# A hybrid encoder layer: chunks of the delta recurrence issued beside the projections of queries and values, with the pages dealt out anew

## The chip, the cores and the metric

The kernel runs on one core of a Trainium2 chip. The metric is the time of one execution of the whole layer in microseconds (us), the median of several runs. Five engines work side by side, each through its own instructions strictly in the order in which they stand: TensorE (PE in the profile, with its weight loads as PEld), VectorE (DVE), ScalarE (ACT), GpSimd (POOL) and SyncE (SP), which here only issues transfers.

## The reference

One encoder layer over 1024 positions of width 1024, in float32. A common RMS norm and one projection feed two mixers: attention over a band of chunks (8 heads of 64) and a gated delta recurrence (4 heads of 128). Their outputs go through an output projection, then a feed-forward network follows.

```python
u    = rms_norm(h, mix_norm_gain)
aq, ak, av, dqkv, dgate, da, db = split(u @ w_in)
o_att = rms_norm(chunked_rel_attention(aq, ak, av, ...), att_out_gain)
dq, dk, dv = split(silu(causal_conv4(dqkv)))
# the recurrence, per head and chunk of the sequence:
#   value, k_cumdecay = triangular solves with (I + strict(beta k k^T * decay))
#   v_new = value - k_cumdecay @ S
#   o     = q_decay @ S + attn_intra @ v_new
#   S     = S * chunk_decay + k_tail^T @ v_new
o_dn = rms_norm(o, dn_out_gain) * silu(dgate)
h = h + concat[o_att, o_dn] @ w_out
h = h + relu(rms_norm(h) @ w_ff1)**2 @ w_ff2
```

The recurrence is serial: chunk c + 1 needs the state S that chunk c leaves.

## The kernel before

The sequence is cut into 8 tiles of 128 positions (the kernel's recurrence also works on 8 chunks of 128). Float32 operands of the large products are split into a high and a low part and multiplied in three passes (`mm3`, L158), so one projection tile `proj_N` or `proj_T` is 24 matmuls of 512 columns.

Generators write the work, and `interleave` (L254) draws from them by weights: each step that a generator yields has a cost in made-up units, and the generator with the least cost per weight so far goes next. This is only the order in which the code is written. A scheduler of the framework then places the instructions on each engine; it may shift them, but within a pool of pages it hands out pages in the order in which the code asked for them.

The mixer has these generators:

- `delta_proj` for the recurrence's queries and values (dq, dv; convolution and SiLU on VectorE, results stored in DRAM), `gate_proj` (g), and `att_proj` for the attention's keys, queries and values (ak, aq, av). In `att_proj`, ScalarE squares a tile, VectorE reduces it, GpSimd takes a power for the norm, VectorE writes the normed tile `qn` (named ak0_n, ak1_n ...), TensorE transposes it (ak0_tp ...), ScalarE and VectorE split it and it is stored. A tile's bank of PSUM (three in `ps_a`) is free again once `qn` is written.
- `delta_prep` (L482): per chunk the products k k^T (d0_m ...), and at the end of all chunks a substitution of 31 steps on VectorE (`td`, `xd`) that inverts the 32x32 diagonal blocks. `xd` and its transposed copy `ad` are stored in DRAM as `x_dr` and `y_dr`.
- `delta_merge` (m0 ... m7) reads them back and builds each chunk's inverse Y by a chain of small products.
- `delta_state` (c0_tpv, c0_pk, c0_pv, c0_pq, c0_pS): the serial part of a chunk. `delta_out` and `delta_fin` (c0_Ltd, c0_tpq, c0_mt, c0_po, c0_tpo): its output.
- `attention` (tiles t00 to t07 for heads 0 to 3, t10 to t17 for heads 4 to 7; a tile is two pairs of heads): `score` (t_sb, t_sa), exponentials on ScalarE, `value` (transposes t_tpb and t_tpa, copies, products t_o), `finish` and `turn`.

Before the change, the first `interleave` (L1263) holds all projections, six of the eight tiles of attention values and `delta_prep`. The second (L1267) holds the attention, the whole recurrence `delta_all` and the last two tiles of values. The output projection `out_proj` follows, with the splits `mixed(0)` tied behind the last square of the recurrence, and the feed-forward network (`ff1`, `ff2`).

All pages of 512 columns live in pools by tag, used in turn: for instance `cv` has 5 pages, `dk` 8, `raw` 2, `x` 2, `on` 2, `u` 24 (the normed input), `wh` and `wl` 10 each.

Of the kernel before, what the change touches and what calls it, by code (L numbers as in the profile page):

```python
# [35 lines left out]
ORDER = "OSMOSMFSOMOSMSL"  # L36
LATE = 2
RS = "a"
NV = 6
WV = 2.5  # L40


@with_exitstack
def hymba_kernel(
# [208 lines left out]

    def interleave(*gens):  # L254

        done = [0.0] * len(gens)
        live = set(range(len(gens)))
        while live:
            i = min(live, key=lambda k: done[k])
            g, w = gens[i]  # L260
            try:
                done[i] += next(g) / w
            except StopIteration:
                live.discard(i)

    def load_block(col, name):
# [128 lines left out]

    def att_proj(u, col, kind, res=None):
        w = load_block(col, f"wa{kind}")
        for t in range(NT):
            n = f"a{kind}{t}"
            ps = proj_N(u[t // TPH], w, t % TPH, n + "_ps")  # L400
            if kind == "v":
                vs = page("jg", n + "_s")
                nc.scalar.mul(vs, ps, r_col[:, t:t + 1])
                nc.sync.dma_start(out=v_dr[t], in_=vs)
                res.append(vs)
                yield 5200
                continue
            sq = page("jq", n + "_sq")
            nc.scalar.activation(sq, ps, AF.Square, scale=r_col[:, t:t + 1])
# [3 lines left out]
            nc.gpsimd.tensor_scalar(r, r, r_col[:, t:t + 1], None, ALU.mult)  # L413
            qn = page("jv", n + "_n")
            q3 = qn.rearrange("p (h d) -> p h d", d=ATT_D)
# [4 lines left out]
            for i in range(4):  # L420
                nc.tensor.transpose(tp[:, i * P:(i + 1) * P], qn[:, i * P:(i + 1) * P], ident)
            hi = page("jg", n + "_h", F32R)
            lo = page("dk", n + "_l", F32R)
# [165 lines left out]
    def delta_state(c, ab, kTs, Ys, D):  # L589

        n = f"c{c}"
        T = "wh" if c + 1 < NT else "jv"
        h4 = slice(4 * c, 4 * c + 4)
# [40 lines left out]
    def delta_out(c, ab, kTs, D):  # L634
        n = f"c{c}"
        T = "wh" if c + 1 < NT else "cv"
        h4 = slice(4 * c, 4 * c + 4)
# [58 lines left out]

    def attention(after):


        def bias_page(tag, name):  # L700
            b = page(tag, name)
            nc.gpsimd.tensor_copy(b[:, 0:1], after[:, 0:1])
            return b
# [17 lines left out]
        def load_keys(g, hf):  # L721
            for i in range(4):
                h = 4 * g + i
                tag = (("dk", "dk"), ("dk", "wl")) if not g else (("u", "wl"), ("dk", "dk"))
                k = page(tag[hf][i // 2], f"ks{g}{hf}{i}", F32R)
                nc.sync.dma_start(out=k.bitcast(F32), in_=k_dr[h // 2, h % 2, :, TH * hf:TH * hf + TH])
                keys[g][hf].append(k)

        def load_values(ts):
            for t in ts:  # L730
                tl = page("dk" if t < 2 else "wl", f"vt{t}")
                nc.gpsimd.tensor_copy(tl[:, 0:1], after[:, 0:1])
                nc.sync.dma_start(out=tl, in_=v_dr[t])
                vt.append(tl)

        def load_rest():
            load_old(0)
            load_values((2, 3))
            load_keys(0, 1)
            load_values(range(4, NT))  # L740
# [154 lines left out]
        for i in range(len(units) + lag + late):  # L895
            if i < len(units):
                g, t, pp = units[i]
                if pp == 0:
                    start(g, t)
                    if (g, t) == (0, 2):  # L900
                        load_rest()
                    if (g, t) == (0, 6):
# [355 lines left out]
    for _ in delta_proj(u, DK, 4, "dk", None, kT, w_dk, first):  # L1258
        pass
    ab = ab_proj(u)  # L1260
    after = []
    values = att_proj(u, AV, "v", after)
    interleave(  # L1263
        (chained(delta_proj(u, DQ, 0, "dq", dq_dr), delta_proj(u, DV, 8, "dv", dv_dr), gate_proj(u),
                 att_proj(u, AK, "k"), att_proj(u, AQ, "q"), first_steps(values, NV)), 1.0),
        (delta_prep(kT, ab), 0.35))
    interleave((attention(after[NV - 1]), 1.0), (delta_all(ab, kT), 2.0), (values, WV))  # L1267
    R = out_proj()
# [51 lines left out]
```

## Time and profile before

| what | us |
|---|---|
| median of the runs (1318.3 to 1320.27) | 1318.68 |
| the profiled execution | 1318.95 |
| its span, first to last instruction | 1317.2 |
| PE busy in the span | 1268.3 |
| DVE busy | 913.0 |
| ACT busy | 543.0 |
| POOL busy | 329.2 |
| start of ak0 (keys' projection) | 214.3 |
| first score of the attention (t00) | 346.7 |
| first score of its second half (t10) | 443.5 |
| first matmul of the output projection | 572.7 |
| start of the feed-forward network's first product | 683.4 |

A matmul's record in the trace is longer than its turn on the array, since matmuls overlap: what one costs is the step from its start to the start of the next. A busy PE may therefore still lose time, by steps that are longer than the shape needs. PEclk is the granted share of TensorE's clock in a stretch, as a fraction of 1.

### The profile page before, as it was taken

How to read it: one execution, taken by the hardware profiler on the slowest of the kernel's cores; microseconds unless marked ns; L12 is line 12 of the kernel's file. 1: busy time of each engine (PE TensorE's matmuls, PEld its weight loads, DVE VectorE, ACT ScalarE, POOL GpSimd, SP SyncE). 2: the span in 40 equal slices, each digit the busy share in tenths (PEclk: the TensorE clock that was granted, in tenths of full speed). 3: DMA queues.
4: the chain of work that ended last, by engine and by line, in shares of the span. 5: the costliest groups of instructions: out<-in, count | busy, mean ns of one | idle time of the engine just before them, and what ended most of it. 6: DMA issues, size and time to landing. Idle time of an engine off the chain costs nothing.

```text
span 1317.2 us, 18003 instructions
## 1 busy us (share of the span) xinstructions
PE 1268.3 (96%) x6686; PEld 1045.9 (79%) x6686; DVE 913.0 (69%) x1379; ACT 543.0 (41%) x902; POOL 329.2 (25%) x513
## 2 busy tenths in 40 slices
PE   8999999999999998989988999999998999999998
PEld 6778878788888877868866888888887788888886
DVE  7899979554056565853549745565559898897988
ACT  7232222232266563744225434444456353333331
POOL 4426542543123364524335000000001000000032
PEclk9999999999999999989988999999999999999999
DMA  7214354666574432115241333323379433403002
GB/s 218 71 43 142 93 157 121 152 161 160 186 208 131 130 101 65 55 51 165 81 160 49 112 96 98 117 92 109 107 266 341 141 136 96 144 32 112 17 32 96
DMA packets 128791, 159.58 MB, mean 121 GB/s; under 512 B 22720, under 2 KB 71872, under 8 KB 128192
## 3 DMA queue, kind: packets, MB, share of 16 engines
q1 hardware_dynamic: 111296, 137.47, 33.7%
q10 hardware_dynamic: 17408, 20.98, 5.1%
q8 instruction: 52, 0.85, 0.3%
q14 instruction: 35, 0.29, 0.1%
HBM read 111.22 MB, written 47.19 MB: 120 GB/s over the span
## 4 chain that ended last, share of the span: by engine, by line
PE 74%; DVE 7%; DMA 2%; issue 2%; POOL 2%; ACT 1%; DVEq 0%; SPq 0%; ACTq 0%; POOLq 0%
PE q L1046 21%; PE p L1132 20%; PE op L163 7%; PE aq_ps L163 3%; PE av_ps L163 3%; PE t_o L850 3%; PE g_ps L163 3%; PE ak_ps L163 2%; DMA t_q<-q_dr 1%; PE t_tpa L840 1%; PE t_tpb L829 1%; PE t_sb L777 1%; PE t_sa L777 1%; DVE h L1013 1%; PE c_po L452 1%
## 5 line engine op out<-in xcount | busy, mean ns | idle before, releaser
L1174 POOL TENSOR_TENSOR y<-y,y 128x1024 f32<-128x1024 f32 x6 | 18.0, 3024 | 279.4 <-DVE y L1170 260.7
L1113 POOL TENSOR_TENSOR y<-y,y 128x1024 f32<-128x1024 f32 x2 | 6.4, 3201 | 294.7 <-DMA y<-h_dr 294.7
L1170 DVE TENSOR_TENSOR y<-y,p 128x1024 f32<-128x1024 f32 x50 | 60.2, 1215 | 12.1 <-PE p L1132 10.7
L793 DVE CUSTOM_DVE_ANT_0 t_pb<-t_sb,biasn 128x256 f32<-128x256 f32 (+1 forms) x64 | 25.6, 402 | 56.7 <-PE t_sb L778 30.9
L163 PE MATMUL op<-mh,wo_h 128*128 128x512 f32 x128 | 50.3, 393 | 0.2 <-DVE t_nm L802 0.2
L163 PE MATMUL op<-ml,wo_h 128*128 128x512 f32 x128 | 50.1, 392 | 0.0
L163 PE MATMUL op<-mh,wo_l 128*128 128x512 f32 x128 | 48.5, 391 | 0.0
L808 ACT ACTIVATE t_pb<-t_pb,t_nm 128x256 f32<-128x256 f32 (+1 forms) x64 | 31.6, 494 | 23.4 <-DVE t_nm L802 15.0
L850 PE MATMUL t_o<-t_ta,vt 128*64 128x128 f32 x240 | 30.1, 302 | 1.8 <-DVE t_ta L843 1.1
L802 DVE CUSTOM_DVE_ANT_0 t_pa<-t_sa,biaso,t_nm 128x384 f32<-128x384 f32 (+2 forms) x48 | 26.3, 548 | 5.5 <-PE t_sa L778 3.3
L163 PEld LDWEIGHTS op<-mh,wo_h 128*128 128x128 f32 x128 | 24.1, 188 | 5.8 <-PE t_tpo L456 0.6
L163 PEld LDWEIGHTS op<-mh,wo_l 128*128 128x128 f32 x128 | 24.0, 188 | 5.2 <-issue 0.2
L954 POOL TENSOR_TENSOR op_q<-op_q 128x512 f32<-128x512 f32 x14 | 19.9, 1422 | 32.7 <-ACT op_q L953 25.2
L777 PE MATMUL t_sb<-ks,t_q 128*128 128x256 f32 (+1 forms) x72 | 23.2, 333 | 5.0 <-DMA t_q<-q_dr 5.0
L163 PEld LDWEIGHTS op<-ml,wo_h 128*128 128x128 f32 x128 | 24.0, 188 | 4.8
L947 DVE TENSOR_TENSOR h<-op,op_x 128x512 f32<-128x512 f32 x16 | 10.8, 686 | 23.7 <-PE op L163 23.7
L298 PE MATMUL dk_ps<-uh,wdk_h 128*128 128x512 f32 x56 | 21.8, 414 | 5.5 <-ACT uh L180 5.5
L840 PE MATMUL t_tpa<-ident,t_pa 128*128 128x128 f32 x120 | 22.4, 293 | 4.5 <-ACT t_on L878 3.2
L811 ACT ACTIVATE t_pa<-t_pa,t_nm 128x384 f32<-128x384 f32 (+2 forms) x48 | 26.4, 550 | 0.1
L163 PE MATMUL g_ps<-uh,wg_l 128*128 128x512 f32 x64 | 25.2, 397 | 0.5 <-POOL wg_l L145 0.5
L850 PEld LDWEIGHTS t_o<-t_ta,vt 128*64 128x64 f32 x240 | 18.1, 144 | 9.5 <-issue 2.2
L163 PE MATMUL dq_ps<-uh,wdq_h 128*128 128x512 f32 x64 | 25.4, 397 | 0.0
(1103 smaller groups left out, 4438.8 us busy)
## 6 DMA issues: line engine op xcount, KB each, us to landing
wa<-in_w_ff_dram SPq DMA_DIRECT2D x32, 512.0 KB
a<-in_w_ff_dram SPq DMA_DIRECT2D x32, 512.0 KB
b<-f_dr SPq DMA_DIRECT2D x32, 512.0 KB
t_q<-q_dr SPq DMA_DIRECT2D x32, 256.0 KB
f_dr<-yy ACTq DMA_DIRECT2D x16, 512.0 KB
f_dr<-zz ACTq DMA_DIRECT2D x12, 512.0 KB
xt<-in_x_t_dram SPq DMA_DIRECT2D x16, 256.0 KB
ks<-k_dr SPq DMA_DIRECT2D x16, 256.0 KB
```

The source lines that it names most:

```text
L163: nc.tensor.matmul(ps, a, b, start=(i == 0), stop=(i == n - 1))
L298: nc.tensor.matmul(ps[ct], a[:, s], b, start=(k + m == 0), stop=(k == NKT - 1 and m == 2))
L777: nc.tensor.matmul(o, q[:, i * P:(i + 1) * P], k[:, c], start=True, stop=False)
L793: nc.vector.tensor_tensor_reduce(sb[:, c], bk[:, c], new[g][pp][:, c], -1.0, 3.0e38, ALU.add, ALU.min, nm[:, 4 + i:5 + i])
L802: nc.vector.tensor_tensor_reduce(sa[e][:, 0:wa], bk[:, 0:wa], old[g][i][:, 384 - wa:384], -1.0, nm[:, 4 + i:5 + i], ALU.add, ALU.min, nm[: ...
L808: nc.scalar.activation(sb[:, c], sb[:, c], AF.Exp, bias=m, scale=-1.0, accum_out=T["sums"][:, 4 + i:5 + i])
L811: nc.scalar.activation(sa[e][:, 0:wa], sa[e][:, 0:wa], AF.Exp, bias=m, scale=-1.0, accum_out=T["sums"][:, i:i + 1])
L840: nc.tensor.transpose(tp[:, js], sa[e][:, js], ident)
L850: nc.tensor.matmul(po[64 * e:64 * e + 64, pp * P:(pp + 1) * P], vt[k0 + j][:, 64 * h:64 * h + 64], (ta[e] if j < na else tb)[:, c:c + P], ...
L1046: nc.tensor.matmul(part(ps, q), l[:, s], r, start=(k + m == 0), stop=(k == 3 and m == 2))
L1132: nc.tensor.matmul(part(ps[q // 2], q % 2), l[:, s], part(r, k), start=(i + k + m == 0), stop=(i + k + m == 4))
L1170: nc.vector.tensor_tensor(y[i][m], y[i][m], ps[m], op)
```

## The change

The first `interleave` now holds `delta_prep` and `delta_all` as one chain with weight 0.4 (before: `delta_prep` alone with 0.35), and it ends as soon as the projections with four tiles of values are through (`until=0`). What is left of the recurrence goes on in the second one beside the attention, with weight 2.0 as before, and the four remaining tiles of values with weight 6 (before: two tiles, 2.5).

Pages are dealt out anew so that the recurrence can live beside the projections: `att_proj` no longer uses `jq`, `jv` and `jg`, which the recurrence needs, but `raw` (squares and values), `cv` (normed keys), `x` (normed queries) and `on` (high parts). Chunks 0 to 4 of the recurrence take their work pages from `dk` and not from `wh`. The first keys of the attention are read into pages of `u`. Some loads move from tile (0, 3) to (0, 2), and pages filled by a transfer are tied to the value tile 3 by a small page `mark`.

```diff
+EARLY = 5
-NV = 6
-WV = 2.5
+NV = 4
+WV = 6
...
-    def interleave(*gens):
+    def interleave(*gens, until=None):
...
                 live.discard(i)
+                if i == until:
+                    return
...
+    mark = mpool.tile([P, 1], F32, name="mark")
+
+    def att_proj(u, col, kind):
...
-                vs = page("jg", n + "_s")
+                vs = page("raw", n + "_s", w=516)[:, 0:512]
                 nc.scalar.mul(vs, ps, r_col[:, t:t + 1])
                 nc.sync.dma_start(out=v_dr[t], in_=vs)
-                res.append(vs)
+                if t == NV - 1:
+                    nc.gpsimd.tensor_copy(mark, vs[:, 0:1])
...
-            sq = page("jq", n + "_sq")
+            sq = page("raw", n + "_sq", w=516)[:, 0:512]
...
-            qn = page("jv", n + "_n")
+            qn = page("cv", n + "_n") if kind == "k" else page("x", n + "_n", w=SEQ)[:, 0:512]
...
-            hi = page("jg", n + "_h", F32R)
+            hi = page("on", n + "_h", F32R)
...
     def delta_state(c, ab, kTs, Ys, D):
-        T = "wh" if c + 1 < NT else "jv"
+        T = "dk" if c < EARLY else "wh" if c + 1 < NT else "jv"
...
     def delta_out(c, ab, kTs, D):
-        T = "wh" if c + 1 < NT else "cv"
+        T = "dk" if c < EARLY else "wh" if c + 1 < NT else "cv"
...
-                tag = (("dk", "dk"), ("dk", "wl")) if not g else (("u", "wl"), ("dk", "dk"))
+                tag = (("u", "u"), ("dk", "wl")) if not g else (("dk", "wl"), ("dk", "dk"))
...
         def load_rest():
-            load_old(0)
-            load_values((2, 3))
-            load_keys(0, 1)
             load_values(range(4, NT))
...
                     if (g, t) == (0, 2):
+                        load_old(0)
+                        load_values((2, 3))
+                        load_keys(0, 1)
+                    if (g, t) == (0, 3):
                         load_rest()
...
-    values = att_proj(u, AV, "v", after)
+    values = att_proj(u, AV, "v")
+    delta = chained(delta_prep(kT, ab), delta_all(ab, kT))
     interleave(
         (chained(delta_proj(u, DQ, 0, "dq", dq_dr), delta_proj(u, DV, 8, "dv", dv_dr), gate_proj(u),
                  att_proj(u, AK, "k"), att_proj(u, AQ, "q"), first_steps(values, NV)), 1.0),
-        (delta_prep(kT, ab), 0.35))
-    interleave((attention(after[NV - 1]), 1.0), (delta_all(ab, kT), 2.0), (values, WV))
+        (delta, 0.4), until=0)
+    interleave((attention(), 1.0), (delta, 2.0), (values, WV))
```

The instructions of TensorE are the same ones, in another order. Three places show it. A number behind a name tells instances apart; `x4` stands for four rows in a row that read alike, and a product of plain float32 operands (c0_pk, m0_p1 and the like) runs as two passes, so that its four rows are eight records in the trace.

The first place is TensorE behind the last matmuls of the fourth key tile (ak3). Before:

```order
L163 MATMUL ak3_ps_2474<-wak_7_h_2295,uh0_7_155 128x512
L163 MATMUL ak3_ps_2474<-wak_7_l_2296,uh0_7_155 128x512
L163 MATMUL ak3_ps_2474<-wak_7_h_2295,ul0_7_156 128x512
L421 MATMUL ak1_tp_2398<-ident_120,ak1_n_2396 128x128 x4
L163 MATMUL ak4_ps_2528<-wak_0_h_2253,uh1_0_157 128x512
```

The same place now:

```order
L164 MATMUL ak3_ps_2695<-wak_7_h_2403,ul0_7_156 128x512
L565 MATMUL m0_p1_2245<-m0_yb_2235,m0_ab_2234 32x32 x4
...
L581 MATMUL m0_tp_2267<-m0_yb_2235,m0_ab_2234 64x64 x4
L589 MATMUL m0_p4_2308<-m0_s1_2236 64x64 x4
L462 MATMUL c0_tpv_2322<-ident_120,c0_jv_2315 128x128 x4
L458 MATMUL c0_pk_2339<-state0_288,kT0_585 128x128 x4
...
L458 MATMUL c0_pv_2461<-c0_jv_2315,m0_yb_2235 128x128 x4
...
L458 MATMUL c0_pq_2479<-state0_288,c0_jq_2314 128x128 x4
...
L458 MATMUL c0_pS_2550<-c0_vn_2466,c0_kt_2320 128x128 x4
L427 MATMUL ak1_tp_2527<-ident_120,ak1_n_2525 128x128 x4
L164 MATMUL ak4_ps_2775<-wak_0_h_2361,uh1_0_157 128x512
```

Between the key tiles 3 and 4 now stand the merge of chunk 0, most of that of chunk 1, and the serial part of chunk 0; before, the first product of a merge came four key tiles later.

The second place is VectorE at the end of the substitution and behind it. Before, ak1_n stood between the last two steps:

```order
L534 TENSOR_TENSOR xd_1599<-xd_1599,td_1600 128x31
L416 TENSOR_TENSOR ak1_n_2396<-ak1_ps_2357,ak1_r_2391 128x512
L125 TENSOR_SCALAR ak2_v_2449<-ak2_ss_2447 128x8
L536 COPY ad_1598<-xd_1599 128x1024
L130 TENSOR_TENSOR ak2_t_2453<-ak2_y_2451 128x8
```

Now:

```order
L540 TENSOR_TENSOR xd_1513<-xd_1513,td_1514 128x31
L542 COPY ad_1512<-xd_1513 128x1024
...
L610 TENSOR_TENSOR c0_jv_2315<-c0_tpv_2322,br_794 128x512
L616 SCALAR_TENSOR_TENSOR c0_jv_2315<-c0_pk_2339,nbr_796,c0_jv_2315 128x128
L616 SCALAR_TENSOR_TENSOR c0_jv_2315<-c0_pk_2339,nbr_796,c0_jv_2315 128x128 x3
L629 TENSOR_TENSOR c0_o_2484<-c0_pq_2479,edec_792 128x512
L422 TENSOR_TENSOR ak1_n_2525<-ak1_ps_2486,ak1_r_2520 128x512
L422 TENSOR_TENSOR ak2_n_2615<-ak2_ps_2576,ak2_r_2610 128x512
```

The tile ak1_n, which frees the bank of ak1, now stands behind c0_o; both take a page of `cv`, and the code asks for that of c0_o first.

The third place is TensorE in the attention's second half, at tile t15. Before:

```order
L452 MATMUL c6_pS_5194<-c6_vn_5109,c6_kt_5005 128x128 x4
...
L777 MATMUL t15_sa1_6184<-ks101_3816,t15_q_6166 128x384
L778 MATMUL t15_sa1_6184<-ks101_3816,t15_q_6166 128x384
L456 MATMUL c7_tpv_5220<-ident_120,c7_jv_5213 128x128 x4
L456 MATMUL c6_tpq_5226<-ident_120,c6_jq_4999 128x128 x4
L829 MATMUL t14_tpb0_6137<-ident_120,t14_pb0_6033 128x128 x4
L840 MATMUL t14_tpa0_6144<-ident_120,t14_pa0_6047 128x128 x3
L452 MATMUL c7_pk_5248<-state1_289,kT1_644 128x128 x4
L840 MATMUL t14_tpa1_6150<-ident_120,t14_pa1_6052 128x128 x3
L456 MATMUL c5_tpo_5312<-ident_120,c5_o_4962 128x128 x4
```

Now:

```order
L780 MATMUL t15_sa1_6186<-ks101_4915,t15_q_6168 128x384
L781 MATMUL t15_sa1_6186<-ks101_4915,t15_q_6168 128x384
L832 MATMUL t14_tpb0_6139<-ident_120,t14_pb0_6035 128x128 x4
L843 MATMUL t14_tpa0_6146<-ident_120,t14_pa0_6049 128x128 x3
L843 MATMUL t14_tpa1_6152<-ident_120,t14_pa1_6054 128x128 x3
L853 MATMUL t14_o_6138<-t14_ta0_6150,vt0_4265 64x128
```

The recurrence is gone from here: its last instruction on TensorE, c7_tpo, now stands at the start of this half (between rows of t07_o), and before it stood at the last one, t17.

More of the change, by code (lines that the diff above doesn't have):

```diff
@@ L394, in ab_proj @@
         return dict(beta=beta, edec=edec, br=br, br2=br2, nbr=nbr, ned=ned, gh=gh.bitcast(F32), gl=gl)
-    def att_proj(u, col, kind, res=None):
+    mark = mpool.tile([P, 1], F32, name="mark")
+    def att_proj(u, col, kind):
         w = load_block(col, f"wa{kind}")
@@ L695, in delta_all, with attention @@
                 yield from gens[k]
-    def attention(after):
+    def attention():
         def bias_page(tag, name):
             b = page(tag, name)
-            nc.gpsimd.tensor_copy(b[:, 0:1], after[:, 0:1])
+            nc.gpsimd.tensor_copy(b[:, 0:1], mark)
             return b
@@ L731, in load_values @@
                 tl = page("dk" if t < 2 else "wl", f"vt{t}")
-                nc.gpsimd.tensor_copy(tl[:, 0:1], after[:, 0:1])
+                nc.gpsimd.tensor_copy(tl[:, 0:1], mark)
                 nc.sync.dma_start(out=tl, in_=v_dr[t])
@@ L1260, in hymba_kernel @@
     ab = ab_proj(u)
-    after = []
-    values = att_proj(u, AV, "v", after)
+    values = att_proj(u, AV, "v")
+    delta = chained(delta_prep(kT, ab), delta_all(ab, kT))
     interleave(
```

## The prediction

> **What bounds the kernel now.** I read the stretches first: busy time by stage, cut at landmarks of TensorE's queue. The columns are the stretch, its length, then busy time (and instructions) of PE, PEld, DVE, ACT and POOL, the granted clock, the DMA share and GB/s.
>
> ```profile
> 214.30:237.80 23.50, 22.34 (x101) 18.20 (x100) 22.07 (x57) 6.19 (x10) 8.27 (x7) 1.00 0.50 134
> 237.80:346.70 108.90, 108.90 (x526) 88.14 (x525) 46.30 (x104) 29.78 (x51) 41.12 (x45) 1.00 0.62 157
> 346.70:443.50 96.80, 95.78 (x884) 81.76 (x882) 51.29 (x184) 58.33 (x177) 36.05 (x104) 1.00 0.60 180
> 443.50:572.70 129.20, 114.20 (x1028) 97.77 (x1027) 80.53 (x237) 72.56 (x208) 62.01 (x154) 0.95 0.25 72
> 572.70:675.60 102.90, 100.15 (x478) 81.17 (x476) 45.18 (x63) 34.03 (x61) 39.30 (x36) 0.98 0.35 112
> ```
>
> The rows are: keys 0 to 3, with the substitution (`td`, `xd`) on DVE; the other keys, queries and values; the attention's first half; its second half; the output projection. TensorE looks busy everywhere, but records of matmuls overlap, so I take its work from steps instead, the timeline of TensorE giving the start of each row:
>
> ```profile
> 549.65 0.60 PE L456 MATMUL c_tpo<-ident,c_o 128*128 128x128 f32 x4
> 550.09 1.06 PE L452 MATMUL c_mt<-c_jq,kT 128*128 128x128 f32 x8
> 550.90 0.36 PE L777 MATMUL t_sa<-ks,t_q 128*128 128x256 f32 x1
> 551.10 0.28 PE L778 MATMUL t_sa<-ks,t_q 128*128 128x256 f32 x1
> 551.22 0.22 PE L777 MATMUL t_sa<-ks,t_q 128*128 128x128 f32 x1
> ...
> 552.45 0.76 PE L850 MATMUL t_o<-t_ta,vt 128*64 128x128 f32 x9
> 552.94 0.27 PE L850 MATMUL t_o<-t_tb,vt 128*64 128x128 f32 x1
> ```
>
> Four transposes step 0.44, so 0.11 each; eight records of a plain float32 product 0.81, so 0.10 (0.11 taken); 256 columns 0.12; nine value products 0.49, so 0.055. A wide matmul of 512 columns steps 0.22 to 0.23, by the rows around the fourth key tile (ak3), which the change touches first:
>
> ```profile
> 237.26 0.39 PE L163 MATMUL ak_ps<-wak_h,uh 128*128 128x512 f32 x1
> 237.48 0.39 PE L163 MATMUL ak_ps<-wak_l,uh 128*128 128x512 f32 x1
> ...
> 237.95 0.60 PE L421 MATMUL ak_tp<-ident,ak_n 128*128 128x128 f32 x4
> 238.30 0.48 PE L163 MATMUL ak_ps<-wak_h,uh 128*128 128x512 f32 x1
> ```
>
> TensorE's rows of each stage times these steps give its work there, in the order before and in the changed one (the recurrence's share in brackets):
>
> - keys 0 to 3, up to the first matmul of ak4 at 238.30: 22.7 (0) before, 30.5 (7.8) after;
> - the rest of the projections, up to t00: 105.2 (1.0), then 121.0 (27.6);
> - first half, up to t10: 79.6 (28.9), then 98.5 (36.9);
> - second half, up to the output projection: 90.6 (43.8), then 48.2 (1.3).
>
> The sum stays at 298. Before, the stages took 24.0, 108.4, 96.8 and 129.2 us, so 1.3, 3.2, 17.2 and 38.6 us are lost. Projections run at TensorE's pace; the attention with the recurrence beside it does not, above all its second half. The change moves recurrence from where 38.6 us are lost to where almost nothing is, so the sum asks how much of that loss goes and how much comes up among the projections.
>
> **The change part by part.**
>
> *The wait behind ak3.* The new order has, between ak3 and ak4, the merge m0 and chunk 0's first products. m0 needs the substitution's result, stored in DRAM and read back. That takes long before as well, but nobody waits for it there. DVE, SP and POOL, from their timelines:
>
> ```profile
> 235.47 0.18 DVE L534 TENSOR_TENSOR xd<-xd,td 128x31 f32<-128x31 f32 x1
> ```
> ```profile
> 236.41 2.77 SPq L539 DMA_DIRECT2D x_dr<-xd  x4
> ...
> 241.84 2.15 SPq L438 DMA_DIRECT2D k_dr<-ak_l  x2
> ...
> 247.92 1.31 SPq L438 DMA_DIRECT2D k_dr<-ak_l  x2
> 249.33 1.21 SPq L550 DMA_DIRECT2D m_s<-y_dr  x2
> ```
> ```profile
> 252.41 2.62 POOL L554 COPY m_yb<-m_s 32x128 f32<-32x128 f32 x8 [2.92 <-DMA m_s<-y_dr]
> ```
>
> `xd` ends at 235.65; SP issues stores and loads until 250.5; POOL's copies start at 252.41, released by the last load, and m0's four of eight are done at 253.7. Nothing on DVE ahead of this is moved, so `xd` ends when it did. On SP the two pairs of `ak_l` stores shown (2.15 + 1.31) fall behind the loads, because their tiles are late themselves: m0 can start at about 250.3. TensorE has its last matmul of ak3 done at 237.95 and then stands at m0_p1 for 12.4 us. Nothing can be put in: ak4 needs a bank of `ak_ps`, and `ak1_n`, which frees one, now stands on DVE behind `c0_o`, the end of chunk 0's first half, since both draw from `cv`. So m0 and chunk 0 must run through as one chain, with no projection in its holes. Its hops on other engines are a copy or an activation of at least the mean of the first row below (ACT, in the second half's groups) for each of m0's four, and DVE's `c_jv` twice and `c_o` (timeline of DVE; the last row is the chunk's state):
>
> ```profile
> L561 ACT COPY m_s<-m_p 32x128 f32<-32x128 f32 x6 | 1.5, 255 | 5.0 <-PE m_p L559 4.9
> ```
> ```profile
> 360.56 0.69 DVE L604 TENSOR_TENSOR c_jv<-c_tpv,br 128x512 f32<-128x512 f32 x1 [4.97 <-PE c_tpv L456]
> ...
> 363.22 1.13 DVE L610 SCALAR_TENSOR_TENSOR c_jv<-c_pk,nbr,c_jv 128x128 f32<-128x128 f32 x4 [0.46 <-PE c_pk L452]
> ...
> 369.85 0.69 DVE L623 TENSOR_TENSOR c_o<-c_pq,edec 128x512 f32<-128x512 f32 x1 [1.88 <-PE c_pq L452]
> ...
> 374.78 1.12 DVE L628 SCALAR_TENSOR_TENSOR state<-state,edec,c_pS 128x128 f32<-128x128 f32 x4 [1.33 <-PE c_pS L452]
> ```
>
> 1.0 + 2.5 = 3.5, with the hops' signals about 4. And a TensorE that stood so long restarts at half clock, as the end of the second half shows (a stretch; TensorE's timeline):
>
> ```profile
> 560.00:566.80 6.80, 4.23 (x16) 2.86 (x16) 3.02 (x8) 2.69 (x7) 4.13 (x13) 0.50 0.00 0
> ```
> ```profile
> 560.86 0.90 PE L840 MATMUL t_tpa<-ident,t_pa 128*128 128x128 f32 x3 [2.98 <-ACT t_on L878]
> 563.47 1.11 PE L456 MATMUL c_tpo<-ident,c_o 128*128 128x128 f32 x4 [1.71 <-POOL c_o L663]
> ```
>
> There 2.98 + 1.71 us of waiting kept the clock at 0.50 for 6.8 us, of which half, 3.4, is the most it can cost, and half of the busy 4.23, about 2, the least; I take 2.6. The term is 12.4 + 4 + 2.6 = **+19**. Low end 12: the chain's hops hidden and no clock loss. High end 26: copies as late as before (3.4 more) and the hops at twice 4 (with 3.4 for the clock, 27 in all, less what the transposes fill).
>
> The Trainium skill's page "TensorE: Matmul & The Clock Gate", Part 1, has the array at half rate after an idle window of about 3.4 us and full again after a busy one of as long. The trace's stretch is twice that length, being broken by a second wait. By the page alone the clock would cost 1.7 us instead of 2.6, and the sum would be 0.9 lower.
>
> *Queries, values and three chunks between them* (ak4 to t00). Each chunk's serial path has DVE's 0.69 + 1.13 + 0.69 + 1.12 = 3.6 us of the rows above. Covered by projection tiles of 24 x 0.227 = 5.4 us of matmuls they cost nothing; where TensorE's row behind is a dependent one, they stand bare. Chunks share `cv`, `dk` and `on` with keys and queries now, so `qn` and `hi` wait for pages as `ak1_n` does. Three chunks bare are 10.9, with one more fall to half clock 14; hidden, 0. Nothing in this stage of the trace shows which, so I take a little over half, **+8**.
>
> *First half* (t00 to t10). The loss of 17.2 falls on 39.8 us of attention and 28.9 of recurrence: 0.25 per us. The recurrence's 36.9 make that +2.0. The first scores' operands come at the end of the moved loads, and this wait is there already (the list of waits, second half: total, times, longest):
>
> ```profile
> PE t_sb L777 <- DMA t_q<-q_dr: 4.0, 2, 2.2
> ```
>
> one more of it is +2: **+4**. Low end −3: the two value tiles that move here from the stage ahead bring 10.9 us of matmuls without waits, which hide 10.9 x 0.25. High end +10: the loss in proportion to all the work, 21.3 (+4), a full 4.0 of the load's waits, and 2 for value rows still waiting for their pages.
>
> *Second half* (t10 to the output projection). Of TensorE's work 48.2 remain: 240 value products x 0.055, 216 transposes and the like x 0.11, 72 score products x 0.117 and 16 x 0.173. What it then waits for is ACT, whose work stays. ACT's timeline gives the steps of two exponentials (each has a read of its sum behind it), its groups in the second half the rest:
>
> ```profile
> 540.95 0.51 ACT L808 ACTIVATE t_pb<-t_pb,t_nm 128x256 f32<-128x256 f32 x1
> ...
> 541.46 0.60 ACT L811 ACTIVATE t_pa<-t_pa,t_nm 128x384 f32<-128x384 f32 x1
> ...
> 542.05 0.58 ACT L477 ACTIVATE c_po<-c_o 128x512 f32<-128x512 f32 x1
> ```
> ```profile
> L808 ACT ACTIVATE t_pb<-t_pb,t_nm 128x256 f32<-128x256 f32 (+1 forms) x31 | 15.3, 494 | 8.4 <-DVE t_nm L802 6.6 <-DVE t_nm L793 1.1 <-DVE t_tot L859 0.3
> L811 ACT ACTIVATE t_pa<-t_pa,t_nm 128x384 f32<-128x384 f32 (+2 forms) x23 | 12.6, 546 | 0.0
> L832 ACT COPY t_tb<-t_tpb 128x512 f32<-128x512 f32 (+1 forms) x16 | 8.9, 558 | 12.5 <-PE t_tpb L829 12.4
> ...
> L845 ACT COPY t_ta<-t_tpa 128x384 f32<-128x384 f32 (+2 forms) x12 | 5.0, 419 | 2.7 <-PE t_tpa L840 2.7
> ...
> L878 ACT ACTIVATE t_on<-t_on 128x512 f32<-128x512 f32 x6 | 3.6, 594 | 0.4 <-DVE t_on L873 0.4
> ...
> L869 ACT COPY t_pb<-t_o 128x256 f32<-128x256 f32 x8 | 2.9, 367 | 3.8 <-PE t_o L850 3.8
> ```
>
> 31 x 0.51 + 23 x 0.59 + 8.9 + 5.0 + 3.6 + 2.9 = 49.8 us. TensorE and ACT have nearly the same load and wait for each other in turn. To 49.8 I add the end, where nothing is left to lay between: the two waits, 4.7, and the half clock, 3.4; and some 2 for the splits of `mixed(0)` on ACT. That is 60 against 129.2, a loss of 11.8 instead of 38.6: **−27**. Low end: ACT's pace and 2 at the end, 52, so −35. High end: the loss rate of the first half on 46.8 of attention, 11.7, with the end's 8 and the splits' 2: loss 21.7, so −17.
>
> The output projection and all behind it keep their rows and order: 0. Sum: 19 + 8 + 4 − 27 = +4, against the profiled execution's 1318.95 (span 1317.2 and 1.75 around it), which lies 0.27 above the median: **1323**.
>
> **The rivals.**
>
> *Faster: the second half at ACT's pace, and chunks hidden among projections.* Speaking for it: ACT's idle time in the second half is in waits for TensorE's transposes and for DVE (L832's 12.5, L808's 8.4), which stand behind the recurrence's rows there and then no longer do. Against it: the same waits come up within a tile. With 52 there and 2 instead of 8 among the projections, the sum is 19 + 2 + 4 − 35 = −10: 1309. The point that decides, with the other terms as above, is a second half of 56 us. The Trainium skill's "Perfetto Trace Analysis", § Optimization Strategy, says that regimes with different contended engines may gain from being interleaved, which would be this case. The rows of the stages bear out that the regimes differ.
>
> *The gap is short.* If m0's operands were back within 5 us of ak3's end, the first term would be 5 and the time 1309. Against it stands SP's row of 14 us of issues and loads, of which the change takes only 3.5 away.
>
> *Slower by more: keys and queries themselves at the recurrence's pace.* Banks and pages freed by steps behind the chunk make each of them wait: the second term at 14, the first at 26, the rest as above, +20 with the first half at +7: 1339. The `ak1_n` place is one such already.
>
> *The change does nothing.* Excluded: the order moves 43 us of TensorE's work out of the second half.
>
> **How the numbers follow.** Forecast 0.45, the slower rival 0.25, the faster one 0.20, the short gap 0.10. The forecast's own range, with the four terms' half widths of 7, 7, 6.5 and 9 taken together as independent (15), is 1308 to 1338; it reaches into both rivals. With these the range is 1302 to 1342. About 0.2%, 2.6 us, is what a measurement can tell from no change. Of the forecast's 0.45, 0.10 lies within that and the rest above; so faster 0.30 (both lower rivals), same 0.10, slower 0.60.
>
> **What the changed profile would show.** Right: an idle time of 10 to 14 us of TensorE ahead of m0_p1, put down to POOL's `m_yb` copies or the `m_s` load, with `xd` ending at 235.6 and a clock of 0.5 behind it; ak4 at 255 to 262; t00 at 372 to 395; 56 to 66 us from t10 to the output projection. Wrong: TensorE's wait under 5 us there, or ak4 ahead of 250; t00 by 365, chunks hidden; the second half at 54 or less, or over 70, where ACT would idle for TensorE as before.

## The result, and the profile after

The changed kernel takes 1355.84 us (median, 1352.29 to 1356.64) against 1318.49 in the same runs: 1.0265 times as long, 95% interval 1.0244 to 1.0287. The forecast was 1323 with a range of 1302 to 1342: slower as forecast, but the range is missed by 14 us and the time by 33. The profiled execution took 1356.64, its span 1354.6.

The stretches of the changed kernel, cut at the same landmarks (ak3's last matmul, ak4, t00, t10, the output projection, the end of its stage):

```profile
237.80:270.10 32.30, 18.82 (x138) 16.20 (x137) 5.83 (x17) 4.88 (x13) 7.20 (x18) 0.57 0.41 94
270.10:404.90 134.80, 130.53 (x788) 106.96 (x786) 64.17 (x142) 41.32 (x76) 68.11 (x113) 0.99 0.49 125
404.90:523.70 118.80, 116.02 (x967) 98.53 (x968) 60.52 (x199) 62.91 (x182) 48.28 (x128) 0.99 0.52 155
523.70:609.20 85.50, 72.82 (x547) 57.28 (x546) 46.52 (x167) 53.44 (x167) 12.90 (x45) 0.86 0.19 50
609.20:713.00 103.80, 99.92 (x478) 80.67 (x476) 46.02 (x64) 34.65 (x62) 39.67 (x37) 0.98 0.35 111
```

What each stage takes beyond the prediction's work by steps ("lost"), before and after:

| stage | before: us, lost | after: us, lost | change of the loss | forecast |
|---|---|---|---|---|
| ak0 to ak4 | 24.0, 1.3 | 56.2, 25.7 | +24.4 | +19 |
| ak4 to t00 | 108.4, 3.2 | 134.8, 13.8 | +10.6 | +8 |
| first half | 96.8, 17.2 | 118.8, 20.3 | +3.1 | +4 |
| second half | 129.2, 38.6 | 85.5, 37.3 | −1.3 | −27 |

The sum is +36.8 of the 37.7 between the two profiled executions; the rest lies in front of ak0 and behind the second half. Three terms came out within their bounds. The fourth, the only gain, did not come: the loss there fell by 1.3 us, not by 27.

**Behind ak3.** TensorE's timeline of the changed kernel, then POOL's and SP's, DVE's, and the clock by stretches:

```profile
237.69 0.39 PE L164 MATMUL ak_ps<-wak_h,ul 128*128 128x512 f32 x1
248.82 0.63 PE L565 MATMUL m_p<-m_yb,m_ab 64*32 64x32 f32 x8 [10.74 <-POOL m_yb L560]
...
254.36 1.11 PE L589 MATMUL m_p<-m_s 64*64 64x64 f32 x8 [0.79 <-ACT m_s L584]
...
269.39 1.06 PE L427 MATMUL ak_tp<-ident,ak_n 128*128 128x128 f32 x4
270.10 0.78 PE L164 MATMUL ak_ps<-wak_h,uh 128*128 128x512 f32 x1
```
```profile
248.14 2.67 POOL L560 COPY m_yb<-m_s 32x128 f32<-32x128 f32 x8 [5.43 <-DMA m_s<-y_dr]
```
```profile
239.35 3.62 SPq L545 DMA_DIRECT2D y_dr<-ad  x4
...
245.81 0.83 SPq L556 DMA_DIRECT2D m_s<-y_dr  x2
```
```profile
265.04 0.69 DVE L629 TENSOR_TENSOR c_o<-c_pq,edec 128x512 f32<-128x512 f32 x1 [5.65 <-PE c_pq L458]
265.65 1.28 DVE L422 TENSOR_TENSOR ak_n<-ak_ps,ak_r 128x512 f32<-128x512 f32 x2
```
```profile
238.00:248.80 10.80, 0.08 (x1) 0.00 (x0) 1.49 (x6) 0.69 (x1) 3.78 (x7) 0.70 0.88 173
248.80:270.10 21.30, 18.55 (x136) 16.20 (x137) 4.17 (x10) 4.20 (x12) 3.42 (x11) 0.50 0.17 53
270.10:272.00 1.90, 1.90 (x7) 1.51 (x6) 1.86 (x5) 0.59 (x1) 0.00 (x0) 0.50 0.00 0
272.00:273.50 1.50, 1.50 (x7) 1.09 (x5) 0.00 (x0) 0.00 (x0) 0.00 (x0) 0.66 0.74 140
273.50:275.00 1.50, 1.50 (x14) 1.27 (x13) 0.00 (x0) 0.73 (x2) 0.53 (x1) 1.00 0.89 221
```

TensorE stands 10.74 us at m0_p1, released by POOL's copies; `ak_n` of two tiles (`x2`) runs directly behind `c_o`, as the order said, and ak4 starts only at 270.10. From 248.8 the clock is at 0.50 for the whole chain of 8.2 us of work, which takes 21.3 us. The full clock comes back only at 273, some 3 us into the projections that follow.

**The second half.** 48.2 us of work by steps take 85.5 us. Cut at t14, before (first two rows) and after:

```profile
443.50:491.50 48.00, 43.45 (x412) 36.96 (x411) 26.21 (x91) 27.81 (x87) 21.63 (x57) 0.96 0.39 106
491.50:572.70 81.20, 70.75 (x618) 60.81 (x618) 54.32 (x147) 44.75 (x122) 40.37 (x98) 0.94 0.17 53
```
```profile
523.70:562.60 38.90, 30.58 (x207) 24.61 (x206) 16.21 (x68) 21.38 (x71) 6.50 (x21) 0.74 0.22 55
562.60:609.20 46.60, 42.24 (x343) 32.67 (x342) 30.32 (x99) 32.06 (x97) 6.40 (x24) 0.96 0.17 46
```

The tiles t10 to t13 have few keys, so few matmuls: 17.8 us of work by steps take 38.9 us, at a mean clock of 0.74. The waits of TensorE in this half (total, times, longest):

```profile
PE t_sb L780 <- DMA t_q<-q_dr: 4.5, 2, 2.4
PE t_tpa L843 <- ACT t_tb L835: 2.3, 2, 2.0
PE t_o L853 <- ACT t_tb L835: 1.5, 2, 0.7
```

### The profile page after: what moved, and what is told of

The parts are those of the page before. It is cut to its first block, busy times and chain, and to the rows that moved or that the text cites. A ratio compares the mean times of both kernels' runs of the same rounds, so it can differ in the third digit from the quotient of the medians.

```text
span 1354.6 us, 17983 instructions
## 1 busy us (share of the span) xinstructions
PE 1288.4 (95%) x6686; PEld 1057.4 (78%) x6686; DVE 910.0 (67%) x1379; ACT 544.8 (40%) x902; POOL 327.5 (24%) x514
## 3 DMA queue, kind: packets, MB, share of 16 engines
q1 hardware_dynamic: 111296, 137.47, 33.1%
## 4 chain that ended last, share of the span: by engine, by line
PE 81%; DVE 8%; DMA 4%; issue 2%; ACT 2%; POOL 1%; SPq 1%; DVEq 0%; ACTq 0%; POOLq 0%
PE q L1053 21%; PE p L1139 20%; PE op L164 6%; PE dq_ps L164 3%; PE av_ps L164 3%; PE aq_ps L164 3%; PE t_o L853 3%; PE dv_ps L164 3%; PE g_ps L164 3%; PE ak_ps L164 2%; DMA t_q<-q_dr 1%; PE t_tpb L832 1%; PE t_tpa L843 1%; PE t_sb L780 1%; PE dk_ps L301 1%
## 5 line engine op out<-in xcount | busy, mean ns | idle before, releaser
L1177 DVE TENSOR_TENSOR y<-y,p 128x1024 f32<-128x1024 f32 x50 | 60.3, 1218 | 12.2 <-PE p L1139 10.9
L811 ACT ACTIVATE t_pb<-t_pb,t_nm 128x256 f32<-128x256 f32 (+1 forms) x64 | 31.7, 496 | 25.7 <-DVE t_nm L805 18.5
L835 ACT COPY t_tb<-t_tpb 128x512 f32<-128x512 f32 (+1 forms) x32 | 17.8, 556 | 24.7 <-PE t_tpb L832 22.5
L853 PE MATMUL t_o<-t_tb,vt 128*64 128x128 f32 x240 | 24.8, 296 | 1.7 <-ACT t_tb L835 1.5
L164 PE MATMUL av_ps<-wav_h,uh 128*128 128x512 f32 x64 | 26.2, 409 | 0.0
```

The source lines that it names most:

```text
L164: nc.tensor.matmul(ps, a, b, start=(i == 0), stop=(i == n - 1))
L811: nc.scalar.activation(sb[:, c], sb[:, c], AF.Exp, bias=m, scale=-1.0, accum_out=T["sums"][:, 4 + i:5 + i])
L853: nc.tensor.matmul(po[64 * e:64 * e + 64, pp * P:(pp + 1) * P], vt[k0 + j][:, 64 * h:64 * h + 64], (ta[e] if j < na else tb)[:, c:c + P], ...
L1177: nc.vector.tensor_tensor(y[i][m], y[i][m], ps[m], op)
```

## The experiments

Each was run against the kernel before on the same chip; ratios are to it, so they compare with the changed kernel's 1.0265. The changed kernel was not run again beside them. Stage times come from the one profiled execution of each. The feed-forward network, whose rows are the same in all, took 628.6 to 634.2 us in these executions, so a few us of a total can be its own. "Lost" is again time beyond the work by steps.

**e1: the recurrence's start later.** A step that does nothing but cost stands between `delta_prep` and `delta_all`, so m0 is written later.

```diff
+    def pause(cost):
+        yield cost
-    delta = chained(delta_prep(kT, ab), delta_all(ab, kT))
+    delta = chained(delta_prep(kT, ab), pause(8000), delta_all(ab, kT))
```

> The recurrence's start (the merge m0 and all behind it) is written later, behind some 1.5 tiles of projections more; m0_p1 then stands on TensorE behind most of ak6 instead of directly behind ak3, and ak4 directly behind ak3. The changed kernel stands dry at m0_p1 for about 11 us and runs the chain m0 to ak1_tp at half clock, 24 us lost in all between ak3 and ak4. Theory: it is the wait for m0's operands through DRAM, with no other row to run. Then ak4 starts at 238 to 240 (270 in the changed kernel), the chain of chunk 0 still loses 4 to 10 us at its new place, and the total is 1336 to 1344. Rival: the chain of m0 and chunk 0 stands bare wherever it is put; then the same 20 us or more are lost around ak6 and ak7 and the total is 1350 or more. The second half of the attention stays at 83 to 88 us by both.

Measured: 1338.71, ratio 1.0119 (1.0092 to 1.0146). ak4 starts at 237.4 and m0_p1, in between ak6's matmuls, at 252.5, without a wait. TensorE's waits in the chain at its new place, from its timeline, and the stretch from ak4 to aq0:

```profile
264.21 0.68 PE L581 MATMUL m_tp<-m_yb,m_ab 64*64 64x64 f32 x8 [0.87 <-ACT m_yb L575]
265.99 0.99 PE L589 MATMUL m_p<-m_s 64*64 64x64 f32 x8 [1.10 <-ACT m_s L584]
...
273.11 2.08 PE L458 MATMUL c_pq<-state,c_jq 128*128 128x128 f32 x8 [0.31 <-ACT c_vn L624]
```
```profile
237.40:280.30 42.90, 39.48 (x247) 32.45 (x245) 20.07 (x48) 13.83 (x29) 22.48 (x32) 0.88 0.72 172
```

At aq0 it has lost 12.9 us since ak0, where the changed kernel had lost 28.7. So the wait for m0's operands with no other row to run was the cause of the larger part; what is left, 11.5 us between ak4 and aq0, is the chain, which still stands bare between ak7 and aq0 with half the clock in its end. That is more than the 4 to 10 expected of it. The total is in the theory's range, and the rival's 20 us at the new place did not come. The second half, expected at 83 to 88, takes 91.6 us, since 4.8 us more of work fell into it.

**e2: queries of the second half in pages of their own ring.**

```diff
-            q = page("x", n + "_q", F32R, w=DM)
+            if g:
+                T["q"] = qs = [page("wh", f"{n}_q{m}", F32R) for m in range(2)]
+                for m in range(2):
+                    for r0 in (0, 64):
+                        nc.sync.dma_start(out=qs[m].bitcast(F32)[r0:r0 + 64], in_=q_dr[t, :, m, g, :])
...
```

> The queries of the second half's tiles (t10 to t17) are read into two pages each of wh, a ring of ten, instead of one of the two wide pages of x, so that a load need not wait until the tile two back has been scored. In the changed kernel the loads of t11 and t12 are on the chain of waits with 4.1 and 4.7 us, and TensorE's clock is at 0.5 to 0.8 from 524 to 556. Theory (the late loads and the half clock behind them make up a third of the loss of the second half): the second half falls from 85.5 to 73 to 79 us, the total to 1343 to 1350. Rival (the attention's own chain from scores over exponentials to values sets the pace): the second half stays at 82 or more, the total at 1352 or more.

Measured: 1348.71, ratio 1.0190 (1.0154 to 1.0226). The second half, cut at t14:

```profile
525.80:559.10 33.30, 28.77 (x207) 22.77 (x206) 16.33 (x68) 21.99 (x72) 6.47 (x21) 0.79 0.26 79
559.10:607.80 48.70, 43.53 (x343) 33.55 (x342) 30.31 (x99) 33.41 (x100) 6.36 (x24) 0.93 0.00 1
```

t10 to t13 lose 5.6 us of their 38.9, the other tiles take 2.1 more: 82.0 in all, which is what the rival said of this stage, while the total was in the theory's range. But the first half takes 123.5 us for the same rows, where it took 118.7, so the attention as a whole is 1.2 us longer. What made the total shorter lies elsewhere: 2.4 us at the start of the output projection, where the clock is 1.00 over the first 10 us and not 0.83, and 4 in the feed-forward network, whose rows are the same; both aren't explained. So the late loads are a part of the first tiles' loss, and the run doesn't show that the whole gains by their coming earlier.

**e3: the recurrence spread over the second half.** Each chunk's first transposes are tied behind the score written last, and the weight beside the attention is lowered.

```diff
+    att_ins = [None]
...
-        four_t(tp, head(dv))
+        if att_ins[0] is None:
+            four_t(tp, head(dv))
+        else:
+            with tc.issue_after(att_ins[0]):
+                four_t(tp, head(dv))
...
-                nc.tensor.matmul(o, q[:, 512 + i * P:512 + (i + 1) * P], k[:, c], start=False, stop=True)
+                att_ins[0] = nc.tensor.matmul(o, q[:, 512 + i * P:512 + (i + 1) * P], k[:, c], start=False, stop=True).ins
...
-    interleave((attention(), 1.0), (delta, 2.0), (values, WV))
+    interleave((attention(), 1.0), (delta, 0.22), (values, WV))
```

> The start of each chunk of the recurrence on TensorE is tied behind the score of the attention that was written last, and the recurrence is written more thinly beside the attention (weight 0.22 instead of 2.0), so that chunks 6 and 7 fall into the second half: its work by steps goes from 48 to about 57, and the last product of the recurrence (c7_tpo) comes 29 us of work later. Theory (attention alone leaves holes and lets the clock drop, 13 us of idle and about 12 of half clock in the second half, which other rows fill): the two halves together fall from 204.3 us to 184 to 195, the total to 1336 to 1347. Rival (the loss sits with each stage and the recurrence brings waits of its own, 38 us in the second half with it and without): the two halves stay at 200 or more, the total at 1351 or more.

Measured: 1355.62, ratio 1.0252 (1.0223 to 1.0281): no difference from the changed kernel that the intervals show. The two halves:

```profile
403.70:515.00 111.30, 109.02 (x889) 91.13 (x890) 52.55 (x181) 58.28 (x174) 34.90 (x97) 0.97 0.54 162
515.00:609.90 94.90, 81.36 (x625) 66.71 (x624) 55.34 (x185) 57.30 (x174) 25.69 (x74) 0.86 0.18 48
```

206.2 us against 204.3, as the rival said: 8.8 us of work went over, and the second half became 9.4 us longer. But in the order of this kernel the state of c6 stands ahead of t10 and that of c7 behind t14, with 16.5 us of work between: t10 to t13 stayed as bare as they were, so this run doesn't tell whether work there is free. That is what e5 asks. For the tiles behind t14 it does tell: with 10.1 us more of work they take 10.1 us more (56.7 for 46.6), so there the recurrence filled no hole.

**e4: the casts mh on POOL.** ACT casts the first half of the mixer's output for the output projection while the second half runs. In the changed kernel four casts stand ahead of a copy that TensorE waits for (ACT's timeline, then TensorE's):

```profile
586.61 2.16 ACT L143 CAST mh<-mixa 128x512 fp32r<-128x512 f32 x4
588.67 0.58 ACT L835 COPY t_tb<-t_tpb 128x512 f32<-128x512 f32 x1
```
```profile
589.31 0.55 PE L843 MATMUL t_tpa<-ident,t_pa 128*128 128x128 f32 x3 [2.00 <-ACT t_tb L835]
```

```diff
-                split(src, hi, lo, nc.scalar, nc.vector)
+                split(src, hi, lo, nc.scalar if hf else nc.gpsimd, nc.vector)
```

> The casts mh of the first half of the mixer's output are made by POOL instead of ACT. In the changed kernel four of them hold ACT for 2.07 us on the chain of waits at 586.7, TensorE waits 2.0 us behind them, and its clock drops for part of the next 5 us. Theory (ACT's extra work ends in TensorE's wait): the second half 3 to 6 us shorter, the total 1350 to 1353. Rival (another wait takes its place, or POOL is late with the casts that the output projection needs first): the second half within 1.5 us of 85.5 or the start of the output projection later, the total 1354 to 1358.

Measured: 1345.92, ratio 1.0182 (1.0156 to 1.0208). The second half, cut at t14:

```profile
524.90:558.70 33.80, 27.49 (x206) 21.79 (x205) 16.23 (x68) 19.23 (x68) 7.73 (x25) 0.85 0.25 63
558.70:602.00 43.30, 40.48 (x342) 31.28 (x341) 30.25 (x99) 29.91 (x93) 8.98 (x28) 1.00 0.18 50
```

77.1 instead of 85.5 us, more than the 3 to 6 expected, and the total is below the theory's 1350: the later tiles now keep a clock of 1.00, and the four other casts, which ran on ACT from 527.10 to 529.27, no longer stand in the narrow tiles, which take 33.8 us for 38.9. In the later tiles TensorE is busy 40.48 of 43.3 us at full clock, and yet the work by steps is 30.4. That is the first sign that the steps taken were too short.

**e5: useless work in the narrow tiles.** 48 products added, into a bank that nobody reads.

```diff
+            if g and t < 4:
+                for r in range(3):
+                    idle = bank(ps_d, f"{n}_idle{pp}{r}")
+                    for e in range(2):
+                        i = 2 * pp + e
+                        nc.tensor.matmul(idle, T["q"][:, i * P:(i + 1) * P], keys[g][0][i], start=(e == 0), stop=(e == 1))
```

> The changed kernel with 48 products of 512 columns added beside the scores of t10 to t13 (six for each pair of heads, into a bank that nobody reads): 48 x 0.227 = 10.9 us of work for TensorE with no operand to wait for. From t10 to t14 the changed kernel takes 38.9 us for 17.8 us of work by steps, at a clock of 0.5 to 0.8. Theory (these narrow tiles leave TensorE idle and its clock low, so other work would be free there): t10 to t14 takes 36 to 43 us, the clock there is over 0.85, the total stays within 4 us of the changed kernel's, 1352 to 1360. Rival (TensorE's own rows take this time): t10 to t14 takes 48 us or more and the total is 1364 or more.

Measured: 1355.1, ratio 1.0292 (1.0232 to 1.0352). t10 to t14:

```profile
520.50:561.70 41.20, 37.36 (x253) 28.86 (x253) 16.50 (x68) 22.16 (x73) 6.50 (x21) 0.92 0.21 52
```

10.9 us of work more cost 2.3 us in this stretch, and the mean clock there rose from 0.74 to 0.92. The tiles behind take 2.1 us more (48.7 for 46.6), so the second half pays 4.4 us for the 10.9. The total doesn't settle it: the interval of the ratio is 1.2 points wide, and in this execution the feed-forward network ran 5.4 us shorter. By its own numbers the theory holds, and its rival's 48 us did not come: the narrow tiles by themselves leave TensorE idle and slow, and work that waits for nothing is largely free there. The recurrence has waits of its own, so it needn't be as cheap. Before, it stood there: t10 to t14 took 48.0 us for 34.4 of work by steps and lost 13.6, where the changed kernel lost 21.1.

**e6: e1, e2 and e4 together.**

> Three edits on the changed kernel together: the recurrence's start later (as in e1), queries of the second half in pages of wh (as in e2), the casts mh on POOL (as in e4). Alone they took about 20, 9 and 12 us off. Theory (three separate causes): about 40 us off, 1314 to 1322, level with the kernel before or a little better. Rival (e2 and e4 take away the same wait, or the next one takes its place): 1325 or more.

Measured: 1325.2, ratio 1.0041 (1.0020 to 1.0062). Alone the three gave 1.46, 0.75 and 0.83 points, 3.04 in sum; together 2.24. The second half takes 74.7 us, 2.4 less than with e4 alone, where e2 alone gave 3.5: e2 and e4 overlap, as the rival said, though only in part. The rest of the difference lies ahead of the second half. Even without these causes the moved recurrence doesn't pay: the kernel before with e4's edit alone (e7, next) is at 0.9949.

**e7: the casts mh on POOL in the kernel before** (e4's edit).

> The kernel before with only the casts mh of the first half of the mixer's output on POOL. ACT ran eight of these casts between 556 and 561 in the kernel before, while TensorE waited 2.98 and 1.71 us at the end of the second half and had half its clock for 6.8 us. Theory (the casts delay ACT's exponentials and copies at the end of the second half in both kernels): the stretch from t16 to the output projection 4 to 9 us shorter, the total 1309 to 1315. Rival (in the kernel before the recurrence's last chunk ends last, whatever ACT does): within 2.5 us of the kernel before.

Measured: 1313.36, ratio 0.9949 (0.9926 to 0.9973): faster than both kernels. The end of the second half, where the kernel before had a wait of 2.98 us and half a clock for 6.8:

```profile
553.00:560.00 7.00, 5.84 (x54) 4.99 (x53) 6.54 (x13) 2.87 (x10) 5.39 (x12) 1.00 0.26 77
560.00:566.00 6.00, 5.38 (x49) 4.25 (x48) 4.95 (x12) 3.14 (x8) 3.90 (x10) 1.00 0.00 0
```

The clock stays at 1.00. t16 to the output projection is only 2.5 us shorter (30.6 for 33.1), less than expected; the output projection up to its last norm gives another 1.8.

**e8: the kernel before with e4's and e2's edit.** Pages of `wh` for the queries move the recurrence ahead and t10 back, so the second half is nearly attention alone, with the projections as before.

> The kernel before with the casts mh on POOL and the second half's queries in pages of wh. This moves the recurrence ahead too: its last product comes at 466 us of work by steps instead of 495, and t10 at 453 instead of 410, so that the second half is nearly attention alone, as in the changed kernel, with nothing changed among the projections. Theory (taking the recurrence out of the second half gains nothing, since the narrow tiles then run bare): not below e7 by more than 3 us, 1310 to 1322. Rival (it was the shared pages and the wait behind the fourth key tile alone that made the change slow, and a second half without recurrence is a gain): 1304 or less.

Measured: 1335.43, ratio 1.0116 (1.0075 to 1.0158), slower even than the theory's range. The attention, cut at t10:

```profile
347.40:515.30 167.90, 148.50 (x1381) 126.81 (x1380) 82.14 (x250) 77.99 (x221) 76.90 (x195) 1.00 0.46 141
515.30:589.60 74.30, 65.19 (x532) 51.24 (x531) 49.68 (x171) 50.29 (x157) 24.91 (x72) 0.98 0.16 48
```

With the work by steps (122.4 and 47.8) the halves lose 45.5 and 26.5, 72 together, where e7's lost 17.7 and 35.7, 53 together. So the second half loses 9 us less without the recurrence, though it keeps most of its loss, and the first half loses 28 more. These 28 have one place, the last 65 us ahead of t10:

```profile
400.00:450.00 50.00, 50.00 (x498) 43.77 (x499) 29.81 (x94) 31.85 (x90) 22.88 (x60) 1.00 0.51 159
450.00:480.00 30.00, 22.20 (x219) 18.84 (x216) 13.23 (x29) 8.16 (x19) 18.86 (x48) 1.00 0.19 59
480.00:515.30 35.30, 23.71 (x214) 20.12 (x213) 15.21 (x32) 7.70 (x16) 20.64 (x43) 1.00 0.26 79
```

Up to 450 TensorE is busy throughout. From there on it has the recurrence all but alone: 36.9 us of work by steps take 65.3, and all of this half's 19.4 us of idle time is there, 6.3 of it behind POOL's `c_att`. The edit didn't only empty the second half, it left the recurrence with nothing beside it. So the two kinds of work lose less where they stand beside each other (53) than where each is left alone for a while (72). The rival's 1304 did not come, but this run doesn't exclude it cleanly: what a second half without the recurrence would gain if the recurrence had other work beside it isn't shown.

## Why the prediction was wrong

**The second half's −27: the work by steps was too small.** The term that failed is the −27, and two steps of its working are wrong. The first is "TensorE's rows of each stage times these steps give its work there", and with it the 48.2 us of work and what I called lost. I took the steps from inside bursts of equal rows. At the start of a burst, and where kinds alternate, they are longer, as two rows of the kernel before show, beside the nine that step 0.49 in the prediction:

```profile
551.48 0.43 PE L850 MATMUL t_o<-t_ta,vt 128*64 128x128 f32 x2
551.84 0.39 PE L777 MATMUL t_sa<-ks,t_q 128*128 128x256 f32 x1
```

Two value products take 0.36 here, 0.18 each and not 0.055. Over the first half of the kernel before, where the prediction's own row showed TensorE busy for 95.78 of 96.80 us at a clock of 1.00, the mean steps from start to start were:

| rows | in each second half | step taken | mean step |
|---|---|---|---|
| value products t_o | 240 | 0.055 | 0.083 |
| t_sb (256 columns and fewer) | 72 | 0.115 | 0.151 |
| t_sa | 64 | 0.128 | 0.162 |
| t_tpb | 60 | 0.110 | 0.118 |

That is 6.7 + 2.6 + 2.2 + 0.5 = 12 us more: by this estimate the second half's attention is some 60 us of TensorE's own time, not 48, and the first half's 17.2 "lost" were mostly such time. It is an upper estimate. A wait shorter than a record, about 0.3 us, leaves no gap, and by the times at which the semaphores were set up to 5 of the 17.2 us can be such waits. I had the row that said so, and put it aside because records overlap. The stage's time that I forecast, 60, is about what its matmuls need with no wait at all.

**The second half's −27: the waits and the clock did not go with the recurrence.** The second step that failed is that of the sum, ACT's 49.8 and behind it only an end of 8.1 (two waits and the half clock) and "some 2 for the splits of `mixed(0)` on ACT". With 60 in place of 49.8 this sum would still give only 70 of the 85.5 us. Of these 85.5, 12.7 are idle, the gaps between TensorE's records; beside them and the 60 some 13 remain. The half clock can account for these (a mean of 0.86 over 85.5 us is 24 us at half rate, worth up to 12), and waits too short to leave a gap for up to 8 of them, by the times at which the semaphores were set; the trace doesn't part the two. Before, the gaps were 15.0, and the mean of 0.95 over 129.2 us is 13 us at half rate, worth up to 6.5.

What the runs show of it: the splits, which I had at 2, were worth 8.4 (e4); with the queries' loads together some 11 (e6's 74.7 for 85.5). That leaves about 15 us over the 60, for which no run has a cause by itself. I had put the beginning of this half at nothing, but there the loss is largest: 21.1 of the 37.3 lie in the narrow tiles t10 to t13, which leave TensorE idle and slow when little stands beside them (e5). The recurrence had been work of another kind in these holes, and beside the attention it lost less than when left alone (e8). ACT's load of 49.8 us was not what set the time (53.44 busy of 85.5); ACT mattered where a cast stood ahead of a copy (e4). The sign that the prediction gave for being wrong, over 70 us here, is what came.

**The wait behind ak3: right in its place and cause, mis-sized inside.** The idle time was 10.74 where I had 12.4: POOL's copies began at 248.14, where my count (252.41 less 3.5) gives 248.9, and m0_p1 started 0.7 us behind their start, where I had counted 1.3 for four of the eight. But hops and clock, 4 + 2.6 in the prediction, were 13.1 (21.3 us for 8.2 of work). I priced the half clock by the 6.8 us that it lasted at the end of the second half; here it lasted from before 248.8 to 273. 24.4 against 19, within the bounds of 12 to 26. Up to aq0, e1 took 15.8 us of loss away. The sign "ak4 at 255 to 262" did not fit the sum that it stands behind: 214.3 with the 30.5 of work, 1.3 lost and the +19 is 265, and t00 follows at 397, not by 395. They came at 270.1 and 404.9.

The Trainium skill's page "TensorE: Matmul & The Clock Gate", Part 1, asks for about 3.4 us of sustained work before the full clock comes back. With dense matmuls from 270.1 on, the trace has 0.50 up to 272.0 and 1.00 from 273.5, which agrees. I had taken from the rule that any 3.4 us of matmuls end the matter, and the chain shows that they don't. But what kept its clock down isn't shown. There are six holes of 0.3 to 0.8 us in it, and yet TensorE's records fill these stretches of it without one:

```profile
254.40:258.70 4.30, 4.30 (x28) 3.91 (x28) 1.13 (x3) 0.38 (x1) 1.68 (x5) 0.50 0.10 31
...
265.90:270.10 4.20, 4.18 (x24) 3.89 (x25) 1.49 (x4) 0.58 (x1) 0.00 (x0) 0.50 0.11 32
```

The holes may have done it, or the small products, whose records cover more than their turns; no run here parts the two.

**Queries, values and three chunks: right in size.** +10.6 for +8, which was a middle between hidden and bare, so some luck is in it. TensorE's idle time in this stage is 4.3 us; the rest are longer steps, 2.7 of them in the small products of the merges, whose steps I had too short as well, and up to 4.9 in the projections (0.248 us a matmul, before 0.235). What of these comes from the pages and what from the chain stays open: the new pages without the recurrence among the projections weren't tried.

**First half: right,** +3.1 for +4. The wait for the queries' load was there, 1.9 us. The other +2 came from the loss rate of 0.25, which was mostly TensorE's own longer steps and not waits; that it fitted is luck. The loads move the other way than the section on the change has it: before, all stood at tile (0, 2); now the last values and the keys of the second half stand at (0, 3).

**The rivals.** The faster one asked for a second half of 56 us or less, and is excluded by 85.5. The short gap is excluded by 10.74. The slower one had the first terms nearly as they came (24.4 for its 26, 10.6 for 14), but took over the −27, and so ended at 1339 instead of 1356. That the loss of a stage could stay with the stage when work leaves it was not among my cases. The −27's bound of −17 came from a loss rate that was itself made of the wrong steps.

## What to carry to other kernels

Take an engine's own time from the sum of start-to-start steps over a stretch in which it doesn't wait, at full clock, not from the step inside a burst: what is called lost otherwise is partly the work's own cost, and goes wherever the work goes. Before work is taken out of a stage to save its waits, ask whether that work was filling them: here the narrow tiles kept their waits, with a lower clock on top, and the recurrence left alone lost 28 of 65 us. Where a serial chain is moved ahead among dense work, look at what stands behind it on the in-order engine and in the rings of pages: a wait that nobody met before (here the way through DRAM) becomes everybody's.

## What the runs showed of the hardware that I had not expected

- A chain of small products with six holes of 0.3 to 0.8 us stayed at a clock of 0.50 for 21 us with TensorE's records busy for 18.55 of them, two stretches of 4.2 and 4.3 us without a hole among them; some 3 us of dense matmuls brought the clock back.
- 10.9 us of useless matmuls in a stretch with a clock of 0.74 cost 2.3 us there and 4.4 in the whole second half; the clock rose to 0.92.
- Eight casts of 0.6 us, moved from ACT to POOL, were worth 0.5% of the kernel before and about 0.8 points of the changed one, though ACT was busy for only 53.44 of 85.5 us in the changed one's second half. I read this as their place in ACT's queue and not their sum; leaving them on ACT at another place wasn't tried.
